# A decoder block in fp32 on one core: the gate of the last 512 output columns moves from the sum into the weights

## The chip, the cores and the metric

The kernel runs on one core of a Trainium2 chip. The metric is the device time of one execution in microseconds (us). The engines that matter here are TensorE (PE), VectorE (DVE), ScalarE (ACT), GpSimd (POOL) and the queue that issues most transfers, SyncE (SP).

## The reference, cut to what matters

One decoder layer with a convolution mixer and an MLP, all in float32, for 256 tokens of width 2048. The change touches only the last line of the MLP:

```python
h = _rms_norm(x, norm2_g[i]) * (1.0 + sc2[:, None, :]) + sh2[:, None, :]
u = jnp.square(jax.nn.relu(h @ mlp_w1[i]))        # 256 x 8192
x = x + (1.0 + g2[:, None, :]) * (u @ mlp_w2[i])  # gate row (1 + g2) per output column
```

The gate `1 + g2` is one row of 2048 numbers, the same for every token, so it may multiply the product `u @ w2` column by column, or the columns of `w2` ahead of the product.

## The kernel before, in words

**Precision.** Each weight tile arrives in SBUF as float32 in a buffer called `raw` (128 x 2048, 1 MB, seven buffers). `split_w` (L225) cuts a tile into two halves of 128 x 1024. For each half ScalarE writes a rounded copy `hi` (L236), and VectorE writes the rest, `lo = raw - hi` (L240). There are six buffers of each, so ScalarE can start a half only when TensorE has done with the one six earlier. TensorE multiplies three times for one product: activations' high part by `hi`, the same by `lo`, activations' low part by `hi` (L310 to L312, and L376 to L378 in `mm_eight`).

**Quarters.** The 8192 hidden columns are worked in four quarters: an "up" stage (`w1`) and a "down" stage (`w2`) each. A quarter's down product has four blocks of 512 output columns (n = 0 to 3). In the last quarter blocks 0 and 1 are put together from seven products of half size (called `eight` jobs, m = 1 to 7) and jobs `down 1` and `down 3`. Blocks 2 and 3 are plain: jobs `down 4` and `down 5` make block 2, `down 6` and `down 7` make block 3, each job one half of the sum over hidden columns. A `down` job has two weight tiles (c = 0, 1), so four halves; an `eight` job has one tile, so two halves. The written order of jobs is `LAST_JOBS`: down 4, eight 1, down 6, eight 5, eight 7, eight 3, down 5, eight 6, eight 2, down 1, eight 4, down 3, down 7. Below they are d4, e1, d6, e5, e7, e3, d5, e6, e2, d1, e4, d3, d7.

**Order of the work.** The program is emitted job by job; the splits of a job are emitted one job ahead of its matmuls, as urgent work. A planner then orders the instructions of each engine by priority and by its own estimate of when each is ready; the hardware runs each engine's list in that order. Some orders are written out by `tc.issue_after`: the tasks of a job (`run_tasks`, L314: finishing sums, squaring the hidden values, half sums) go behind the last `lo` and `hi` emitted, and the adds of the `eight` jobs on whole raw tiles (L356) go behind the last `lo` before them.

**Hidden values.** The squared hidden values `u` of a quarter are split in the same way: ScalarE writes the high part (L251), VectorE the low part (L254). d5 needs the last of them.

**The gate.** The gate row lies in `cb` (the tile `cond`), spread over all partitions, from a transfer that is issued at 890.1 us. For blocks 0 to 2 `finish` (L446) adds the sum in PSUM to `y` (what earlier quarters gave), multiplies by the gate row (L458) and lets a GpSimd-issued DMA add it to the output (L460). Block 3 is the one with `n == ADDED`. Its `y` is multiplied by the gate and joined with the residual ahead of time (`scale_y`, L1166 and L1167); `finish` then multiplies the PSUM sum by the gate (L458), adds it to `y` (L462) and stores `y` through SP (L463). It runs once for each half of the tokens, t = 0 and t = 1. The last job d7 finishes t = 0 before it begins t = 1.

Of the kernel before, what the change touches and what calls it, by code (L numbers as in the profile page):

```python
# [12 lines left out]
ALU = mybir.AluOpType  # L13
PSUM = bass.MemoryType.PSUM

P = 128
# [4 lines left out]
QUARTERS = FF // D  # L21
# [60 lines left out]
ADDED = 3  # L82
# [5 lines left out]
def conv_block(ctx: ExitStack, tc: tile.TileContext, x, vec, dwq, c_row, mod_r, mod_t, mod_c, w_first, w_in, w_out, w1, w2, out):  # L88
    nc = tc.nc
# [41 lines left out]
    for i in range(2):  # L131
        p = ps.tile([P, 2, 2 * T], F32, name="mm", bufs=2)
        for n in range(2):
            at = 8 * i + 4 * n
            nc.tensor.matmul(p[:, n, :], ones[0:1, :], cond[0:1, at : at + 4, :], start=True, stop=True)
        nc.scalar.activation(cond[:, 8 * i : 8 * i + 8, :].rearrange("p k n -> p (k n)"), p.rearrange("p a b -> p (a b)"), AF.Silu)
    cb = cond.rearrange("p k n -> p (k n)")
    nc.scalar.activation(cz[:, :, 3], col("c", 0, KT), AF.Silu)
    state = {"used": 0}
# [74 lines left out]
    def take(key, hold=False):  # L214
        assert order[state["used"]] == key, (order[state["used"]], key)
        state["used"] += 1
        if not hold:
            release(home(key))
        return raw.pop(key)
# [5 lines left out]
    def split_w(key, engine, w=None):  # L225
        w = take(key) if w is None else w
        if key[:2] == ("up", 0) and key[2] < UNSCALED:
            shown[key] = w
        halves = []
        for h in range(2):  # L230
            ks = slice(h * HALF, (h + 1) * HALF)
            hi = wts.tile([P, HALF, P], F32R, name="hi", bufs=6)
            lo = wts.tile([P, HALF, P], F32R, name="lo", bufs=6)
            with tc.issue_after(state["silu"]) if key == ("out", 1, 1) else ExitStack():
                with tc.issue_after(state["part"]) if key[0] == "in" and "part" in state else ExitStack():
                    state["w_hi"] = nc.scalar.activation(hi, w[:, ks, :], AF.Copy).ins  # L236
            by = nc.vector if key == ("in", HELD, 0) and h == 0 else engine
            with tc.issue_after(state["e_end"]) if key[0] == "out" and engine is nc.vector else ExitStack():
                with tc.issue_after(state["part_sum"]) if key[0] == "in" and "part_sum" in state else ExitStack():
                    end = by.tensor_tensor(lo, w[:, ks, :], hi.bitcast(F32), op=ALU.subtract)  # L240
            if by is nc.gpsimd:
                state["pool"] = end.ins
            else:
                state["w_lo_of"] = state.get("w_lo_of", [end.ins])[-1:] + [end.ins]
                state["w_lo"] = end.ins
            halves.append((hi, lo))
        parts[key] = halves
# [75 lines left out]
    def split_seven(q, m):  # L323
        name = {1: "x", 5: "x", 6: "x", 4: "x", 7: "w", 3: "z", 2: "y"}[m]
        if m == 1:
            for n in "xw":
                for c in range(2):
                    chain[n, c] = take(("seven", q, n, c), True)
        if m in (7, 2):
            for c in range(2):  # L330
                n = "z" if m == 7 else "y"
                chain[n, c] = take(("seven", q, n, c), True)
        for c in range(2):
            if m in PLUS:
                with tc.issue_after(state["w_lo_of"][c]):
                    nc.vector.tensor_tensor(chain[name, c], chain[name, c], chain[PLUS[m], c], op=ALU.add)
            if m in (6, 4):
                release()
        for c in range(2):
            with behind(c):  # L340
                split_w(("seven", q, m, c), nc.vector, chain[name, c])
            if m in (7, 4):
                release()
            if c == 0:
                run_tasks()
# [4 lines left out]
    def split_eight(q, m):  # L350
        name = OPERAND[m]
        for n in {1: "xw", 7: "z", 2: "y"}.get(m, ""):
            chain[n] = take(half_tile(q, n), True)
        if m in PLUS:
            with tc.issue_after(state["w_lo"]):
                nc.vector.tensor_tensor(chain[name], chain[name], chain[PLUS[m]], op=ALU.add)  # L356
        if m in (6, 4):
            release()
        if m == 1:
            run_tasks()  # L360
        split_w(("eight", q, m), nc.vector, chain[name])
        if m in (7, 4):
            release()
        if m != 1:
            run_tasks()
# [80 lines left out]
    def finish(n, t, cs, p):  # L446
        at = slice(512 * n + cs.start, 512 * n + cs.stop)
        s = y[:, t, at]
        g = two().rearrange("p a t -> p (a t)")[:, cs]
        with tc.issue_after(state["y_end"].ins) if "y_end" in state else ExitStack():  # L450
            if (n, t) in MORE:
                m, op = MORE[n, t]
                nc.vector.tensor_tensor(g, p, kept_of[m], op=op)
                p = g
            if n < ADDED:
                nc.vector.tensor_tensor(g, p, s, op=ALU.add)
                p = g
            state["y_end"] = nc.vector.tensor_tensor(g, p, cb[:, at], op=ALU.mult)  # L458
        if n < ADDED:
            nc.gpsimd.dma_start(rows_out[:, t, at], g, accum_op=ALU.add)  # L460
            return
        state["y_end"] = nc.vector.tensor_tensor(s, s, g, op=ALU.add)  # L462
        nc.sync.dma_start(rows_out[:, t, at], s)  # L463

    def residual_out(n, b):
        with tc.issue_after(state["load"].ins):
# [246 lines left out]
    def ps_two():  # L713
        return ps.tile([P, 2, T], F32, name="acc", bufs=2)

    def two():
        return tmp.tile([P, 2, T], F32, name="two", bufs=6)
# [53 lines left out]
    for job in jobs:  # L771
        n = quota.get(job, 0)
# [5 lines left out]
        if job[:2] in LATE_GATE:  # L778
            n = LATE_GATE[job[:2]][job[2]]
# [25 lines left out]
    def splits(job):  # L805
        if job[0] == "eight":
            with urgent():
                split_eight(*job[1:])
            return
        if job[0] == "seven":  # L810
            with urgent():
                split_seven(*job[1:])
            return
        for c in range(2):
            if job + (c,) in parts_early:
                continue
            on_pool = job[0] == "in" or job in POOLED
            with urgent(), behind(c):
                split_w(job + (c,), nc.gpsimd if on_pool else nc.vector)
            if c == 0:  # L820
                state["next_hi"] = state["w_hi"]
                if job[0] in ("up", "down"):
                    with urgent():
                        run_tasks()
# [10 lines left out]
    p = ps.tile([P, 512], F32, name="small", bufs=1)  # L835
    for k2 in range(HALF):
        s = two()
# [4 lines left out]
        for j in range(2):  # L842
            g = (2 * k2 + j) % 4
            nc.tensor.matmul(p[32 * g : 32 * g + 32, 0:T], ones[:, 0:32], s[:, j, :], start=k2 < 2, stop=k2 >= HALF - 2)
    mods(by_col(0))
    with urgent():
        part = two()[:, 0, :]
        nc.scalar.activation(part, p[:, 0:T], AF.Copy)
        p = ps.tile([P, 512], F32, name="row", bufs=1)
# [8 lines left out]
    for _ in range(2):  # L858
        p = ps.tile([P, 2, 2 * T], F32, name="mm", bufs=2)
# [52 lines left out]
    for k in range(KT):  # L912
# [4 lines left out]
        if c == 0:  # L917
            n = two()
# [7 lines left out]
        if last:  # L926
            w = take(("first", k))
# [241 lines left out]
    rows_out = out.rearrange("(t p) d -> p t d", t=2)  # L1169
# [5 lines left out]
    for n, job in enumerate(jobs):  # L1175
# [51 lines left out]
        if kind == "out" and i > 0:  # L1227
            p = ps_two()
        elif not by_tokens(job):
            p = ps.tile([P, 2, 2 * T], F32, name="mm", bufs=2)  # L1230
# [38 lines left out]
        if n == KT - 3:  # L1269
            for key in cols_in:  # L1270
                w = take(key)
# [7 lines left out]
        if kind == "in":  # L1279
# [86 lines left out]
            for k2 in range(HALF):  # L1366
# [17 lines left out]
                with urgent():  # L1384
                    nc.gpsimd.tensor_tensor(e, pair_of(cvs, k2), spread(mu), op=ALU.subtract)
                    state["e_end"] = nc.vector.tensor_tensor(e, e, spread(r), op=ALU.mult).ins
                    for c in range(2):
                        k = 2 * k2 + c
# [17 lines left out]
        if kind == "out":  # L1406
# [4 lines left out]
            with urgent():  # L1411
                for c in range(2):
                    k = 2 * i + c
# [10 lines left out]
            a = two()  # L1424
            for c in range(2):
                k = 2 * i + c
# [27 lines left out]
        elif kind == "up":  # L1454
# [5 lines left out]
            if plain:  # L1460
                with urgent():
                    t2 = evac(p)
                    a = two()
                    nc.vector.tensor_tensor(t2, t2, spread(r2), op=ALU.mult)
                    for c in range(2):
                        at = 2 * i + c
# [19 lines left out]
        else:  # L1486
# [16 lines left out]
            if job == ("down", QUARTERS - 1, 3):  # L1503
                with tc.issue_after(state["w_lo"]):
                    for t in range(2):
                        at = slice(1536, 2048)
# [3 lines left out]
            for t, cs, p in sums.pop((kind, i // 2)):  # L1510
                at = slice(512 * (i // 2) + cs.start, 512 * (i // 2) + cs.stop)
                s = y[:, t, at]
# [69 lines left out]
```

## Time and profile before

| | us |
|---|---|
| median of 3 runs (lowest, highest) | 1067.75 (1067.61, 1067.9) |
| span of the profiled execution, first to last instruction | 1065.8 |
| TensorE busy in the span | 1048.6 (98%) |
| VectorE busy | 911.9 (86%) |
| ScalarE busy | 609.0 (57%) |
| GpSimd busy | 220.2 (21%) |

Of the profiled execution the span is the time that is known; the median of the runs is 1.95 us above it. A span counts from the first to the last instruction that the profiler records. Times in timelines are from the start of the span. Instructions of one engine that follow each other without a pause may be drawn together (x4).

### The profile page before, as it was taken

The page shows a single profiled execution, that of the slowest core. Times are in us where ns is not written, and L with a number is a line of the kernel's source. Part 1 is how long each engine was busy: PE and PEld are TensorE (multiplying, and loading weights), DVE is VectorE, ACT ScalarE, POOL GpSimd, SP SyncE. Part 2 cuts the span into 40 slices and gives each one's busy share as a digit, 9 for nine tenths or more (in the row PEclk, how much of TensorE's full clock was granted, in tenths as well). Part 3 has the DMA queues.
Part 4 walks back from the last instruction along what each step waited for, and adds up shares of the span by engine and source line. Part 5 has one row for each costly group of instructions (what it writes and reads, how often), then busy time and mean ns, then how long its engine had stood idle before and what let it go on. Part 6 is the DMA issues. An engine that isn't in the chain of part 4 may idle for free.

```text
span 1065.8 us, 15587 instructions
## 1 busy us (share of the span) xinstructions
PE 1048.6 (98%) x5844; PEld 867.4 (81%) x5844; DVE 911.9 (86%) x1176; ACT 609.0 (57%) x841; POOL 220.2 (21%) x153
## 2 busy tenths in 40 slices
PE   6999999999999999999999999999999999999998
PEld 3888886678699998888888888888888888888886
DVE  5767789998766889878879899899999899899896
ACT  4111298866775587444546575745566744657751
POOL 0000078989689262000000000000000000000001
PEclk8999999999999999999999999999999999999999
DMA  9999997997999977999994998693989795899753
GB/s 383 420 420 421 415 419 310 359 397 261 382 401 404 405 247 285 324 334 313 324 359 178 340 269 284 238 382 109 383 241 308 252 331 183 289 304 341 203 146 60
DMA packets 154334, 331.01 MB, mean 311 GB/s; under 512 B 88465, under 2 KB 114321, under 8 KB 119313
## 3 DMA queue, kind: packets, MB, share of 16 engines
q1 hardware_dynamic: 153248, 328.30, 84.8%
q0 software_dynamic: 864, 1.57, 1.1%
q8 instruction: 46, 0.75, 0.3%
q14 instruction: 30, 0.25, 0.1%
q10 hardware_dynamic: 146, 0.13, 0.0%
HBM read 313.71 MB, written 17.83 MB: 311 GB/s over the span
## 4 chain that ended last, share of the span: by engine, by line
PE 83%; DMA 10%; DVE 5%; ACT 1%; issue 1%; SPq 0%; DVEq 0%; ACTq 0%
PE mm L312 12%; PE mm L310 12%; PE mm L311 12%; DMA raw<-mod_c 9%; PE mm L268 6%; PE mm L269 3%; PE acc L265 3%; PE acc L264 3%; PE acc L266 3%; PE mm L1090 2%; PE row L576 2%; PE acc L485 2%; PE acc L486 2%; PE acc L484 1%; DVE raw L669 1%; DVE lo L240 1%
## 5 line engine op out<-in xcount | busy, mean ns | idle before, releaser
L236 ACT ACTIVATE hi<-raw 128x1024 fp32r<-128x1024 f32 x374 | 384.8, 1055 | 258.2 <-PE mm L312 127.6
L240 DVE TENSOR_TENSOR lo<-raw,hi 128x1024 fp32r<-128x1024 f32 x313 | 371.7, 1219 | 52.6 <-ACT hi L236 51.4
L240 POOL TENSOR_TENSOR lo<-raw,hi 128x1024 fp32r<-128x1024 f32 x61 | 153.6, 2549 | 31.1 <-ACT hi L236 31.1
L669 DVE SCALAR_TENSOR_TENSOR raw<-raw,cond 128x2048 f32<-128x2048 f32 x50 | 117.7, 2356 | 27.0 <-DMA raw<-mod_c 26.9
L460 POOL DMA_DIRECT2D out<-two x6 | 5.4, 902 | 641.6 <-DVE two L458 632.3
L311 PE MATMUL mm<-lo,u 128*128 128x512 f32 x320 | 124.5, 389 | 0.0
L312 PE MATMUL mm<-hi,u 128*128 128x512 f32 x320 | 124.0, 389 | 0.0
L310 PE MATMUL mm<-hi,u 128*128 128x512 f32 x320 | 123.8, 389 | 0.0
L312 PE MATMUL mm<-hi,hl 128*128 128x512 f32 x288 | 112.1, 389 | 0.0
L311 PE MATMUL mm<-lo,hl 128*128 128x512 f32 x288 | 112.0, 389 | 0.0
L310 PE MATMUL mm<-hi,hl 128*128 128x512 f32 x288 | 112.0, 389 | 0.0
L969 DVE SCALAR_TENSOR_TENSOR acc<-u,v,acc 128x256 f32<-128x256 f32 x230 | 91.5, 482 | 0.0
L268 PE MATMUL mm<-hl,hi 128*128 128x512 f32 x224 | 80.0, 401 | 0.0
L311 PEld LDWEIGHTS mm<-lo,u 128*128 128x128 f32 x320 | 60.1, 188 | 12.6
L312 PEld LDWEIGHTS mm<-hi,u 128*128 128x128 f32 x320 | 60.1, 188 | 12.5
L310 PEld LDWEIGHTS mm<-hi,u 128*128 128x128 f32 x320 | 60.1, 188 | 12.4
L873 PE MATMUL mm<-two,first 128*128 128x256 f32 x240 | 57.0, 392 | 8.5 <-ACT two L931 8.5
L264 PE MATMUL acc<-hl,hi 128*128 128x256 f32 x224 | 63.4, 283 | 0.0
L265 PE MATMUL acc<-hl,hi 128*128 128x256 f32 x224 | 63.4, 283 | 0.0
L266 PE MATMUL acc<-hl,lo 128*128 128x256 f32 x224 | 63.4, 283 | 0.0
L312 PEld LDWEIGHTS mm<-hi,hl 128*128 128x128 f32 x288 | 54.1, 188 | 11.3
L311 PEld LDWEIGHTS mm<-lo,hl 128*128 128x128 f32 x288 | 54.1, 188 | 11.2
(381 smaller groups left out, 2059.2 us busy)
## 6 DMA issues: line engine op xcount, KB each, us to landing
raw<-w SPq DMA_DIRECT2D x128, 1024.0 KB, 7.3
raw<-mod_c SPq DMA_DIRECT2D x64, 1024.0 KB, 9.7
raw<-mod_r SPq DMA_DIRECT2D x28, 1024.0 KB, 8.8
raw<-w_in SPq DMA_DIRECT2D x16, 1024.0 KB, 10.5
raw<-w_out SPq DMA_DIRECT2D x16, 1024.0 KB, 8.0
first<-w_first SPq DMA_DIRECT2D x15, 1024.0 KB, 19.8
u<-kept SPq DMA_DIRECT2D x24, 512.0 KB, 7.6
flat<-two SPq DMA_DIRECT2D x30, 256.0 KB, 6.9
```

The lines of the kernel that those rows point to most:

```text
L236: state["w_hi"] = nc.scalar.activation(hi, w[:, ks, :], AF.Copy).ins
L240: end = by.tensor_tensor(lo, w[:, ks, :], hi.bitcast(F32), op=ALU.subtract)
L264: nc.tensor.matmul(out_p, w, m[:, 0:T], start=begin, stop=False)
L265: nc.tensor.matmul(out_p, w, m[:, T : 2 * T], start=False, stop=False)
L266: state["mm_end"] = nc.tensor.matmul(out_p, lo[:, k % HALF, :], m[:, 0:T], start=False, stop=end)
L268: nc.tensor.matmul(p[:, c, :], hi[:, k % HALF, :], m, start=(k == 0), stop=(k == KT - 1))
L310: nc.tensor.matmul(p, p_hi, hi, start=begin, stop=False, skip_group_check=shared)
L311: nc.tensor.matmul(p, p_hi, lo, start=False, stop=False, skip_group_check=shared)
L312: nc.tensor.matmul(p, p_lo, hi, start=False, stop=end, skip_group_check=shared)
L669: end = nc.vector.scalar_tensor_tensor(w, w, 1.0, cb, op0=ALU.mult, op1=ALU.mult, accum_out=acc)
L873: step = nc.tensor.matmul(held[n][:, c, :], w[:, 2 * n + c, :], h, start=k == 0 and c == 0, stop=k == KT - 1, skip_group_check=True)
L969: end = nc.vector.scalar_tensor_tensor(out, s, w, acc, op0=ALU.mult, op1=ALU.add)
```

## The change

In `split_w` the four tiles of d6 and d7 in the last quarter (`key[2] // 2 == ADDED`) get one more VectorE instruction for each half: the half of the raw tile is multiplied, in place, by the gate row of block 3 (two stretches of 512 columns in a half of 1024), ahead of `hi` and `lo`. That makes eight new instructions of 128 x 1024. In `finish`, block 3 loses the multiplication: it adds PSUM to `y` in one instruction and stores it. `scale_y` stays, and so do blocks 0 to 2.

```diff
         halves = []
+        gated = key[:2] == ("down", QUARTERS - 1) and key[2] // 2 == ADDED
         for h in range(2):
             ks = slice(h * HALF, (h + 1) * HALF)
+            if gated:
+                m = w[:, ks, :].rearrange("p (k a) n -> p k (a n)", a=4)
+                gate_row = cb[:, 512 * ADDED :][:, None, :].to_broadcast([P, 2, 512])
+                nc.vector.tensor_tensor(m, m, gate_row, op=ALU.mult)
             hi = wts.tile([P, HALF, P], F32R, name="hi", bufs=6)
             lo = wts.tile([P, HALF, P], F32R, name="lo", bufs=6)
...
         at = slice(512 * n + cs.start, 512 * n + cs.stop)
         s = y[:, t, at]
+        if n == ADDED:
+            with tc.issue_after(state["y_end"].ins):
+                state["y_end"] = nc.vector.tensor_tensor(s, p, s, op=ALU.add)
+            nc.sync.dma_start(rows_out[:, t, at], s)
+            return
         g = two().rearrange("p a t -> p (a t)")[:, cs]
         with tc.issue_after(state["y_end"].ins) if "y_end" in state else ExitStack():
             if (n, t) in MORE:
                 m, op = MORE[n, t]
                 nc.vector.tensor_tensor(g, p, kept_of[m], op=op)
                 p = g
-            if n < ADDED:
-                nc.vector.tensor_tensor(g, p, s, op=ALU.add)
-                p = g
-            state["y_end"] = nc.vector.tensor_tensor(g, p, cb[:, at], op=ALU.mult)
-        if n < ADDED:
-            nc.gpsimd.dma_start(rows_out[:, t, at], g, accum_op=ALU.add)
-            return
-        state["y_end"] = nc.vector.tensor_tensor(s, s, g, op=ALU.add)
-        nc.sync.dma_start(rows_out[:, t, at], s)
+            nc.vector.tensor_tensor(g, p, s, op=ALU.add)
+            state["y_end"] = nc.vector.tensor_tensor(g, g, cb[:, at], op=ALU.mult)
+        nc.gpsimd.dma_start(rows_out[:, t, at], g, accum_op=ALU.add)
```

## Rows read from the trace of the kernel before

**Rows 1.** The page, part 2: busy tenths in 40 slices of the span
```profile
PE   6999999999999999999999999999999999999998
DVE  5767789998766889878879899899999899899896
```

**Rows 2.** Stages: from:to, length, busy us (instructions) by engine, granted clock, DMA
```profile
975.00:990.00 15.00, 15.00 (x68) 12.39 (x67) 13.77 (x21) 7.67 (x10) 0.00 (x0) 1.00 0.92 289
1000.00:1010.00 10.00, 10.00 (x46) 8.29 (x45) 8.61 (x8) 9.65 (x14) 0.00 (x0) 1.00 0.51 160
1040.00:1050.00 10.00, 10.00 (x46) 8.29 (x45) 9.50 (x13) 2.79 (x3) 1.75 (x2) 1.00 0.42 52
1050.00:1061.00 11.00, 11.00 (x49) 8.85 (x48) 4.33 (x7) 0.00 (x0) 1.75 (x2) 1.00 0.45 73
```

**Rows 3.** The chain that ended last, its end: start us, us, what
```profile
1060.88 0.24 PE mm L312
...
1061.14 0.70 DVE two L458
...
1061.87 0.69 DVE x L462
```

**Rows 4.** SP's timeline at the end, and the landing of that transfer
```profile
1062.59 0.36 SPq L463 DMA_DIRECT2D out<-x  x1
out<-x SPq DMA_DIRECT2D x1, 256.0 KB, 2.1
```

**Rows 5.** DVE groups by shape, 960 to 1067: count, busy us, mean ns, idle before
```profile
L240 DVE TENSOR_TENSOR lo<-raw,hi 128x1024 fp32r<-128x1024 f32 x44 | 52.3, 1218 | 6.0 <-ACT hi L236 5.7
L458 DVE TENSOR_TENSOR two<-mm,cond 128x512 f32<-128x512 f32 x2 | 1.4, 692 | 6.7 <-PE mm L312 6.7
```

**Rows 6.** DVE's timeline, 981 to 1014: start us, us, what [idle before, releaser]
```profile
981.98 0.69 DVE L428 TENSOR_TENSOR hl<-v,hl 128x512 fp32r<-128x512 f32 x1 [0.36 <-ACT hl L427]
...
984.77 1.23 DVE L240 TENSOR_TENSOR lo<-raw,hi 128x1024 fp32r<-128x1024 f32 x1 [0.29 <-ACT hi L236]
986.30 3.94 DVE L240 TENSOR_TENSOR lo<-raw,hi 128x1024 fp32r<-128x1024 f32 x3 [0.31 <-ACT hi L236]
990.16 2.28 DVE L356 TENSOR_TENSOR raw<-raw 128x2048 f32<-128x2048 f32 x1
...
999.33 4.63 DVE L240 TENSOR_TENSOR lo<-raw,hi 128x1024 fp32r<-128x1024 f32 x4
...
1012.28 1.28 DVE L254 TENSOR_TENSOR u<-two,u 128x512 fp32r<-128x512 f32 x2
```

**Rows 7.** ACT's timeline: a `hi` of d6, and two of d5
```profile
985.21 1.06 ACT L236 ACTIVATE hi<-raw 128x1024 fp32r<-128x1024 f32 x1 [0.47 <-PE mm L312]
...
1006.73 1.99 ACT L236 ACTIVATE hi<-raw 128x1024 fp32r<-128x1024 f32 x2
```

**Rows 8.** PE's timeline: first `lo` of d6, of e7; u's low part in d5
```profile
990.67 0.39 PE L311 MATMUL mm<-lo,u 128*128 128x512 f32 x1
...
1004.05 0.39 PE L377 MATMUL acc<-lo,hl 128*128 128x512 f32 x1
...
1015.61 0.62 PE L312 MATMUL mm<-hi,u 128*128 128x512 f32 x2
```

**Rows 9.** SP's timeline and landing time: the load of d6's second tile
```profile
965.41 0.33 SPq L212 DMA_DIRECT2D raw<-w  x1
raw<-w SPq DMA_DIRECT2D x1, 1024.0 KB, 10.3
```

**Rows 10.** DVE's and PE's timelines: the last `lo` of d7, and its use
```profile
1045.91 1.23 DVE L240 TENSOR_TENSOR lo<-raw,hi 128x1024 fp32r<-128x1024 f32 x1 [0.47 <-ACT hi L236]
...
1054.37 0.39 PE L311 MATMUL mm<-lo,u 128*128 128x512 f32 x1
```

**Rows 11.** POOL's timeline: the last adding transfer, and its landing
```profile
1055.87 0.88 POOL L460 DMA_DIRECT2D out<-two  x1 [3.59 <-issue]
out<-two POOLq DMA_DIRECT2D x1, 256.0 KB, 4.1
```

## The prediction

> **What bounds the kernel now.** I read the page's slices first: TensorE is at 9 tenths in every slice but the first and the last, and VectorE runs at 8 and 9 tenths near the end [rows 1]. Then the stages. From 975 to 1061 us TensorE is busy for the whole length of each one, at its upper clock level (granted clock 1.00), so no microsecond is lost there to a wait, and only something that makes TensorE wait can add time [rows 2]. VectorE has little room: 13.8 of 15 us, 8.6 of 10, 9.5 of 10, and it gets room only after 1050 (4.3 of 11) [rows 2]. Third, the end of the chain of waits: TensorE's last matmul ends at 1061.12; VectorE then multiplies PSUM by the gate row from 1061.14 and adds into `y` from 1061.87 [rows 3]; the store is issued at 1062.59 and lands 2.1 us later [rows 4]. So the time is TensorE's work to 1061.12 and a tail of two VectorE instructions and a transfer.
>
> **The change part by part.**
>
> *The tail loses one instruction.* Between the starts of the multiply and the add lie 1061.87 - 1061.14 = 0.73 us [rows 3]. In the new kernel the add reads PSUM and `y` and can start at 1061.14 itself. An instruction of that shape with an operand in PSUM takes 692 ns [rows 5], the add from SBUF 0.69 [rows 3], so the add gets no longer. The store and its landing move forward by the same amount. The term is -0.73 us. The same happens to t = 0, five microseconds earlier, off the path. What is late next is the last adding transfer of block 1, issued at 1055.87 and landed 4.1 us later, at about 1060 [rows 11]; the store's landing moves from 1064.7 to 1064.0, so some 4 us remain between them.
>
> *Eight multiplies are added to VectorE.* No row has this instruction, a multiply in place with a row read twice. The nearest is the `lo` subtraction: the same engine, 128 x 1024, two float32 operands from SBUF, 1218 ns [rows 5]. In a row of four, three starts take 4.63 - 1.23 = 3.40 us, so one instruction more costs 1.14 [rows 6]. The far bounds are nothing for all eight, if they fall into idle time, and 8 x 1.23 = 9.8 us, if each lay on the path. I take 1.14 each: 4.56 us for d6 and 4.56 for d7. None of it is on the path unless a `lo`, a `hi` or a low part of `u` reaches TensorE late. So I follow the lag.
>
> *d6.* Before, VectorE did d6's four `lo` from 984.77, and the next add (e5's) began at 990.16 [rows 6]: 5.39 us for 4 x 1.14 = 4.56, so 0.83 idle, with 0.29 in front of it. ScalarE's `hi` waited for TensorE's buffers [rows 7], so these gaps can be filled by multiplies. The gap of 0.36 at 981.98 [rows 6] can take the first multiply as well, because the load is there: issued at 965.41 for the second tile, landed 10.3 us later, at 975.7 [rows 9]. What is left is a lag of 4.56 - 0.83 - 0.29 - 0.36 = 3.1 us, or 3.4 if the first multiply does not use that gap. Behind the last `lo` of d6 stand e5's add, e5's `lo`, e7's add and so on, an order written into the code, and all move by this lag. Now the slack. d6's first `lo` ended at 986.0 and was wanted at 990.67 [rows 6, 8]: one multiply and one round trip ahead of it, 2.3 us, does not reach 4.7. e7's first `lo` ended at 999.33 + 1.23 = 1000.56 and was wanted at 1004.05 [rows 6, 8]: slack 3.49, just above the lag. The low part of `u` in d5 ended at about 1012.28 + 0.68 = 1012.96 and was wanted at 1015.61 [rows 6, 8]: slack 2.65. Part of the lag should be gone by then, but little, because ScalarE is busy 9.65 of 10 us from 1000 to 1010 [rows 2] and d5's `hi` [rows 7] come late with it. With 2.7 to 3.1 us of lag left, TensorE would wait 0.05 to 0.45 us. Against that, the planner sees the later `u` and has matmuls of d5 that need only `hi`, `lo` and the high part of `u`; I count 0.1 us. The ends are 0 and, with nothing absorbed, the second rival's price.
>
> The Trainium skill, in VectorE: DVE Perf Modes, section "The DRAIN you can't avoid", says that the next VectorE instruction doesn't start until the pipe of the one in front is empty. By that eight instructions would cost 1.23 each instead of 1.14, 0.7 us more for d6's stretch, a lag of 3.8 and a wait of some 1.15 us at `u`: 1067.75 - 0.73 + 1.15 = 1068.2, slower than before. The four `lo` that follow each other in 4.63 us disagree with it [rows 6]; I leave it as a part of the second rival, one chance in twenty.
>
> *d7.* Its four multiplies come after d5's stretch, when the lag has had ScalarE's idle time to shrink (2.8 of 10 us busy from 1040 on) [rows 2]. The last `lo` of d7 ended at 1045.91 + 1.23 = 1047.14 and is wanted at 1054.37 [rows 10]: slack 7.2, above all four multiplies (4.56) and what may remain of d6's. The sums of blocks 0 and 1 that stand between them get later by up to 4.6 us; VectorE is idle for 6.7 us after 1050, between the two last waits for TensorE [rows 5], and takes them there. Cost 0; without that cover the last adding transfer would land at 1060 + 4.6 = 1064.6, beside the end of the store.
>
> *Moved transfers.* The raw buffers of d6 come free 3 us later, so SP's next loads of weights go out later by up to that. These are for d1 and later jobs. The add and the store of the last block stay on the same engines, and the fewer `two` buffers only make room.
>
> *Sum*: the span 1065.8 - 0.73 + 0.1 = 1065.2. The runs lie 1.95 above the span, so 1067.75 - 0.63 = 1067.1.
>
> **The rivals.**
>
> 1. *The forecast*: 1067.1, from 1066.8 (no wait; a store that lands 0.2 earlier) to 1067.6 (a wait of 0.5).
>
> 2. *VectorE's lag reaches TensorE at e7 and d5* (the other side). With no gap used, all 4.56 us of d6's multiplies arrive at e7: a wait of 4.56 - 3.49 = 1.07, and then 4.56 - 2.65 - 1.07 = 0.84 at d5's low part of `u`, together 1.9. That gives 1067.75 - 0.73 + 1.9 = 1068.9. It decides from a lag of 2.65 + 0.73 = 3.4 us at `u`: there the gain is gone. For it speaks VectorE's full stretch and ScalarE's in rows 2; against it the gaps beside d6's `lo` and the planner's freedom in the order of matmuls.
>
> 3. *A multiply at the head of VectorE's list waits for its load.* ScalarE's `hi` used to be the first to need a raw tile. If the planner believes that the load of 965.41 lands sooner than the 10.3 us it took [rows 9] and places the multiply there, VectorE stands for some microseconds with everything behind it, on top of the lag: 2 us more than in the second rival, 1068.9 + 2 = 1070.9. Against it: half sums and transposes emitted ahead fill VectorE until 981, past the landing.
>
> 4. *The tail gain is taken back by another end.* If the sums of blocks 0 and 1 slip by 4.6 us or more, the last adding transfer ends where the store ended: 1067.75, no change. The 4 us between the two landings and VectorE's idle time after 1050 speak against it. [...]
>
> **How the numbers follow.** Chances: forecast 0.60, second rival 0.24, third 0.06, fourth 0.10. The predicted time is the forecast's 1067.1. The range runs from 1066.6 (the forecast's low end with the spread of the runs, 0.15 to each side) to 1069.0, which takes in the fourth rival and the second at its full price; the third and the worst of the second are left out. A difference of 0.2% is 2.1 us, about what a measurement can tell from no change: faster means below 1065.6, slower above 1069.9. No case reaches the first: 0.02. The second comes from the third rival and waits above 2.9 us in the second: 0.07. Within: 0.91.
>
> **What the new profile would show.** The tail: one VectorE add with PSUM as operand right behind the last matmul and nothing between it and the store; if that is missing, the first term is wrong. Eight multiplies of about 1.2 us on `raw`, four before about 993 and four between 1019 and 1045. e5's add 3 us later than now against TensorE's place; TensorE without idle time from 975 to its last matmul, or with a wait for VectorE at e7's first `lo` or d5's low part of `u`: a total over 0.73 us there makes the second rival right. A VectorE wait on a transfer in front of a multiply shows the third. If TensorE's last matmul ends where it does now and the time still doesn't fall, it is the fourth. A matmul count or a pace other than today's would make the whole argument wrong.

## The result, and the profile after

The change made the kernel slower. Its median is 1074.53 us (1073.99 to 1075.92, 5 runs) against 1067.75 (1067.34 to 1067.9, 5 runs) in the same job: a ratio of 1.0065, 95% interval 1.0054 to 1.0076. The forecast was 1067.1 us, with a range up to 1069.0. The profiled execution has a span of 1072.2 us where the kernel before had 1065.8, so 6.4 us are to be found in the two traces.

The groups on VectorE, 960 to 1075 us (count, busy us, mean ns, idle before), correspond to [rows 5]:

```profile
L245 DVE TENSOR_TENSOR lo<-raw,hi 128x1024 fp32r<-128x1024 f32 x44 | 51.8, 1214 | 1.0 <-ACT hi L241 1.0
L236 DVE TENSOR_TENSOR raw<-raw,cond 128x1024 f32<-128x1024 f32 x8 | 9.4, 1211 | 3.4 <-DMA raw<-w 3.4
...
L456 DVE TENSOR_TENSOR x<-mm,x 128x512 f32<-128x512 f32 x2 | 1.4, 692 | 4.5 <-PE mm L317 4.5
```

The eight multiplies (L236) are there and as long as a `lo`. The last block has one instruction with PSUM as operand (L456), and nothing stands between it and the store. In the second row is something that the kernel before did not have: 3.4 us in which VectorE waited for the load of weights. The same stages as in [rows 2]:

```profile
975.00:990.00 15.00, 12.45 (x53) 9.62 (x53) 15.00 (x21) 3.59 (x5) 0.00 (x0) 1.00 0.99 318
1000.00:1010.00 10.00, 10.00 (x46) 8.28 (x45) 9.79 (x9) 8.19 (x12) 0.00 (x0) 1.00 0.55 177
1040.00:1050.00 10.00, 10.00 (x46) 8.29 (x45) 9.98 (x11) 5.25 (x5) 0.00 (x0) 1.00 0.21 26
1050.00:1061.00 11.00, 11.00 (x51) 9.09 (x50) 9.67 (x15) 0.00 (x0) 1.75 (x2) 1.00 0.35 44
```

TensorE lost time in one stage only, the first: 53 matmuls in place of 68 [rows 2]. Behind it TensorE is full again, and VectorE, which had 6.7 of 11 us free after 1050, has 1.3. Two places follow from these rows.

**TensorE in d4.** VectorE's timeline (start us, us, what, [idle before, releaser]), then TensorE's:

```profile
970.45 0.68 DVE L1166 TENSOR_TENSOR pad<-acc,pad 128x512 f32<-128x512 f32 x1
974.55 2.36 DVE L236 TENSOR_TENSOR raw<-raw,cond 128x1024 f32<-128x1024 f32 x2 [3.42 <-DMA raw<-w]
976.82 0.69 DVE L259 TENSOR_TENSOR u<-cz,u 128x512 fp32r<-128x512 f32 x1
...
980.96 0.68 DVE L259 TENSOR_TENSOR u<-shz,u 128x512 fp32r<-128x512 f32 x1
```
```profile
981.70 0.50 PE L317 MATMUL mm<-hi,u 128*128 128x512 f32 x1 [2.46 <-DVE u L259]
```

Up to 970.45 both executions agree to 0.01 us. Then the order in the instruction list decides: the first two multiplies of d6 stand ahead of the low parts of `u` that d4 needs, and their load hasn't landed. In the kernel before, these two low parts began at 971.32 and 975.46; now at 976.82 and 980.96, 5.5 us later: 3.42 of waiting and 2.27 for two multiplies, less the 0.20 that VectorE waited there before. The two in the kernel before:

```profile
971.32 0.69 DVE L254 TENSOR_TENSOR u<-cz,u 128x512 fp32r<-128x512 f32 x1 [0.20 <-ACT u L251]
...
975.46 0.68 DVE L254 TENSOR_TENSOR u<-shz,u 128x512 fp32r<-128x512 f32 x1
```

TensorE waits for the low part. The last block's add, which follows the last matmul at once, begins at 1064.35; VectorE's first instruction behind that matmul began at 1061.14 before [rows 3]. That is 3.2 us, and the fifteen missing matmuls at 0.23 each (3.4) agree as far as such counts can tell. The trace marks 2.46 of it as one wait, at the second low part; the rest is a short wait at the first and the starts behind both.

**Behind the last matmul.** The last adds of VectorE, and GpSimd's issues of the adding transfers:

```profile
1051.92 0.68 DVE L466 TENSOR_TENSOR two<-two,cond 128x512 f32<-128x512 f32 x1
...
1058.43 0.69 DVE L466 TENSOR_TENSOR two<-two,cond 128x512 f32<-128x512 f32 x1
...
1064.35 0.69 DVE L456 TENSOR_TENSOR x<-mm,x 128x512 f32<-128x512 f32 x1 [4.52 <-PE mm L317]
```
```profile
1052.97 0.87 POOL L467 DMA_DIRECT2D out<-two  x1 [13.04 <-DVE two L466]
1057.96 0.89 POOL L467 DMA_DIRECT2D out<-two  x1 [4.13 <-DVE two L463]
1062.25 0.87 POOL L467 DMA_DIRECT2D out<-two  x1 [3.40 <-issue]
1066.74 0.88 POOL L467 DMA_DIRECT2D out<-two  x1 [3.62 <-issue]
```

All four sums of blocks 0 and 1 are done by 1059.12, but their transfers leave one by one, 4.3 to 5.0 us apart, the last at 1066.74, after the store's add. From it to the end of the span are 5.46 us; before, the last one was issued at 1055.87 [rows 11] and the store ended the kernel. The span now ends 7.85 us after the start of the last block's add, before 4.66 after the start of its multiply: 3.2 us more, where the removed instruction should have made it 0.73 less. The chain of waits names it, towards its end:

```profile
1058.85 3.39 issue
...
1062.26 0.86 POOL out L467
1063.12 3.60 issue
```

So 6.4 = 3.2 (TensorE) + 3.2 (end), as the two traces are compared at the last add. On the path at the end is the chain of transfers alone, and the two parts are not independent: that chain starts with block 0's first sum, and VectorE's standstill in d4 makes that late as well. In the kernel before, that sum and the issue behind it were:

```profile
1040.69 0.68 DVE L458 TENSOR_TENSOR two<-two,cond 128x512 f32<-128x512 f32 x1
```
```profile
1041.73 0.87 POOL L460 DMA_DIRECT2D out<-two  x1 [10.23 <-DVE two L458]
```

The experiments test whether these are two causes, and what each is.

### The profile page after: what moved, and what is told of

The parts are those of the page before. It is cut to its first block, busy times and chain, and to the rows that moved or that the text cites. A ratio compares the mean times of both kernels' runs of the same rounds, so it can differ in the third digit from the quotient of the medians.

```text
span 1072.2 us, 15587 instructions
## 1 busy us (share of the span) xinstructions
PE 1049.4 (98%) x5844; PEld 867.4 (81%) x5844; DVE 918.7 (86%) x1182; ACT 607.8 (57%) x841; POOL 220.0 (21%) x153
## 4 chain that ended last, share of the span: by engine, by line
PE 73%; DVE 11%; DMA 9%; issue 3%; ACT 2%; SPq 0%; POOL 0%; POOLq 0%; DVEq 0%; ACTq 0%
PE mm L315 10%; PE mm L316 10%; PE mm L317 10%; DMA raw<-mod_c 7%; PE mm L273 6%; DVE lo L245 4%; PE mm L274 3%; PE acc L270 3%; PE acc L269 3%; PE acc L271 3%; PE mm L1094 2%; PE row L580 2%; DVE raw L673 1%; DVE raw L341 1%; PE acc L489 1%
## 5 line engine op out<-in xcount | busy, mean ns | idle before, releaser
L315 PEld LDWEIGHTS mm<-hi,hl 128*128 128x128 f32 x288 | 54.1, 188 | 11.3
L317 PEld LDWEIGHTS mm<-hi,hl 128*128 128x128 f32 x288 | 54.1, 188 | 11.3
```

Source lines behind the costliest of these rows:

```text
L315: nc.tensor.matmul(p, p_hi, hi, start=begin, stop=False, skip_group_check=shared)
L317: nc.tensor.matmul(p, p_lo, hi, start=False, stop=end, skip_group_check=shared)
```

## The experiments

All times are medians with lowest and highest, the ratio is to the kernel before in the same job (1067.65 to 1067.79 there). It rests on all runs and not on the two medians, so it can differ a little from theirs.

| run | what differs from the changed kernel | us | ratio, 95% |
|---|---|---|---|
| tail_only | no multiplies | 1066.91 (1066.65 to 1068.2) | 0.9994 (0.9985 to 1.0003) |
| only6 | multiplies on d6 alone | 1070.87 (1068.61 to 1071.97) | 1.0024 (1.0014 to 1.0033) |
| only7 | multiplies on d7 alone | 1070.59 (1069.64 to 1071.83) | 1.0026 (1.0016 to 1.0035) |
| hold6 | d6's each behind the newest `lo` | 1074.46 (1074.09 to 1075.12) | 1.0065 (1.0052 to 1.0077) |
| hold67 | as hold6; d7's behind block 0's sums | 1071.64 (1071.27 to 1074.95) | 1.0047 (1.0034 to 1.0061) |
| hold6u | d6's behind `u`'s low parts | 1073.23 (1069.99 to 1075.2) | 1.0046 (1.0033 to 1.006) |
| hold6u7 | as hold6u; d7's behind block 0's sums | 1067.71 (1067.29 to 1069.92) | 1.0001 (0.9992 to 1.001) |
| poolmul | multiplies on GpSimd | 1080.98 (1078.88 to 1081.66) | 1.0118 (1.0104 to 1.0131) |
| scratch | GpSimd's ring of transfers 1024 bytes, not 512 | 1075.67 (1074.32 to 1077.82) | 1.0077 (1.0064 to 1.0089) |
| before_shift | kernel before, ring and padding of scratch | 1073.2 (1073.11 to 1075.15) | 1.0057 (1.0043 to 1.007) |
| before_pad | kernel before, padding of scratch alone | 1072.97 (1072.73 to 1073.11) | 1.005 (1.0033 to 1.0067) |

**tail_only.**

```diff
-        gated = key[:2] == ("down", QUARTERS - 1) and key[2] // 2 == ADDED
+        gated = False
```

> The changed kernel without its eight multiplies (so block 3 of the last quarter gets no gate in this quarter's sum; that part is left out). VectorE's work ahead of the tail is then that of before. Theory and rival agree on the tail term: one VectorE instruction fewer behind the last matmul, 1067.75 - 0.73 = 1067.0 us, the last matmul ending at 1061.1 as before. If the gain is below 0.3 us, the store was not what ended the kernel before.

1066.91, that is 0.76 below the kernel before of its job (1067.67), though the interval of the ratio takes in 1. VectorE's timeline at the end shows the add alone behind the last matmul, and the span is 1065.2, so the store ends the kernel 3.9 us after the start of the add (4.66 after the start of the multiply before):

```profile
1061.32 0.69 DVE L456 TENSOR_TENSOR x<-mm,x 128x512 f32<-128x512 f32 x1 [4.75 <-PE mm L317]
```

The gain of the tail is there in the trace, and its 0.76 by the medians is near the 0.73 that was counted; the eight multiplies cost all the rest.

**only6 and only7.** The multiplies of one job are left out; only7 has `== 7` in this line.

```diff
-        gated = key[:2] == ("down", QUARTERS - 1) and key[2] // 2 == ADDED
+        gated = key[:2] == ("down", QUARTERS - 1) and key[2] == 6
```

> Only tile d6's weights are multiplied by the gate row; d7's are not, so half of the last block's product lacks the gate row: the output differs, the rest of the work is as after. Theory (two causes that add up: d6's first multiply waits 3.4 us for its load in front of u's low parts, +3.2 us for TensorE; d7's four multiplies push block 0's sums back and with them the chain of adding transfers, +3.9 us at the end less 0.7): the wait of 3.4 us and TensorE's 2.5 us in d4 are still there, the last matmul ends at 1064.3, the sums come some 4.6 us earlier than in after, and the store ends the kernel again: 1070.2 us. Rival (the sums are late because of the lag from d6, not of d7's multiplies): the adding transfers still end the kernel: 1072.5 us or more.

> Only tile d7's weights are multiplied by the gate row; d6's are not, so half of the last block's product lacks the gate row: the output differs, the rest is as after. Theory: nothing stands ahead of u's low parts in d4, TensorE ends at 1061.1 as before; block 0's first sum comes 4.6 us later than before, at 1045.3, and four adding transfers 4.4 us apart from there are issued by 1059.7 and end no later than the store: 1067.0 us (up to 1068). Rival (d7's four multiplies alone make the sums so late that the adding transfers end the kernel, as in after): 1070 us or more.

Each job's multiplies cost some 3 us by themselves: 3.1 for d6's and 2.8 for d7's over the 1067.79 of their job, each with the tail's gain of 0.76 already in it. Without it, 3.84 + 3.56 = 7.4, and the changed kernel has 6.78 + 0.76 = 7.54 (medians in all cases): two causes whose times add up. In only6 TensorE waits for `u`'s low part, and the last adding transfer is issued at 1057.90, early enough that the store ends the kernel; this was the theory. The wait differs between the two profiles with the landing of the load: VectorE waited 2.44 us here and 3.42 in the changed kernel. That may be why only6's runs spread over 3.4 us; this profile is of one of its shortest (1069.05). TensorE's waits in only6, in total, times, longest:

```profile
PE mm L317 <- DVE u L259: 1.9, 1, 1.9
```

For only7 the theory named the right mechanism and gave it the wrong size; the rival was right. TensorE waits for nothing from 960 on, and yet the kernel is 2.8 us slower. VectorE's first sum of block 0, then GpSimd's issues:

```profile
1049.00 0.68 DVE L466 TENSOR_TENSOR two<-two,cond 128x512 f32<-128x512 f32 x1
```
```profile
1050.04 0.87 POOL L467 DMA_DIRECT2D out<-two  x1 [13.46 <-DVE two L466]
1054.65 0.89 POOL L467 DMA_DIRECT2D out<-two  x1 [3.74 <-DVE two L466]
1058.90 0.87 POOL L467 DMA_DIRECT2D out<-two  x1 [3.37 <-issue]
1063.22 0.88 POOL L467 DMA_DIRECT2D out<-two  x1 [3.45 <-issue]
```

The sum that I expected at 1045.3, the old 1040.69 plus four multiplies, comes at 1049.00. The multiplies account for 4.6 of the 8.3 us. The rest is order: the planner now places the last three `lo` instructions (3.4 us) and `scale_y`'s first two instructions (L1170, at 1047.79, 1.2 us) ahead of that sum, where they stood behind it. That is 9.2 us of work in all, a part of which went into idle time. From the sum on, four transfers follow each other at the pace of GpSimd's queue.

**hold6 and hold67.** Two attempts to give the multiplies another place.

```diff
+                with tc.issue_after(state["w_lo"]) if key[2] == 2 * ADDED else ExitStack():
                     nc.vector.tensor_tensor(m, m, gate_row, op=ALU.mult)
```

In hold67 d6's are as here, and d7's are issued after `state["y_end"].ins`, which is the last of block 0's two sums at that point.

> The changed kernel with the four multiplies of d6 held behind e1's last lo on VectorE, so that none stands at the head of VectorE's list while its load is still under way. Theory (two causes: a multiply that waits 3.4 us for its load, and sums of blocks 0 and 1 so late that the adding transfers, one every 4.4 us, end the kernel): TensorE's wait at d4 goes (last matmul at 1061.1 to 1061.5 instead of 1064.3), but the sums stay late, so the end falls by about 3.4 us, not by 6.8: 1071 us, from 1070 to 1072. Rival (VectorE has no room for 9.1 us of new work, wherever it stands, and TensorE waits for the lag): TensorE still ends at 1063 or later, 1073 us or more.

> As hold6, and d7's four multiplies are held behind the sums of block 0 (behind the gate multiply of its second token half). Same instructions, same count. Theory: TensorE does not wait, block 0's sums are done by about 1046 us and the last adding transfer ends by about 1065, beside the store: 1067.0 to 1068.5 us. Rival (no room on VectorE): d7's lo then come too late for TensorE, which waits 3 us or more before its last job: 1071 us or more.

hold6 took the load wait away and won nothing: the theory's number fell. This order sets `lo` and multiply in turn, and each `lo` now waits for ScalarE's `hi`, which waits for the multiply in front of it. VectorE's timeline, then what TensorE waited for (lines are one higher in this kernel):

```profile
991.12 1.22 DVE L237 TENSOR_TENSOR raw<-raw,cond 128x1024 f32<-128x1024 f32 x1
993.47 1.23 DVE L246 TENSOR_TENSOR lo<-raw,hi 128x1024 fp32r<-128x1024 f32 x1 [1.12 <-ACT hi L242]
...
998.09 2.28 DVE L362 TENSOR_TENSOR raw<-raw 128x2048 f32<-128x2048 f32 x1
```
```profile
PE acc L382 <- ACT hi L242: 1.7, 1, 1.7
PE acc L383 <- DVE lo L246: 0.8, 1, 0.8
PE row L383 <- DVE lo L246: 0.7, 1, 0.7
```

e5's add comes at 998.09, 7.9 us later than before [rows 6], and TensorE loses 3.2 us between 1000 and 1010: the place of the prediction's second rival, at a higher price. hold67 keeps this loss (its three waits add up to 3.2 as well) and yet is 2.8 us faster than hold6. There the first sum of block 0 ends at 1044.86, and the last adding transfer is issued at 1063.29, not 1067.26. The end can therefore be mended apart from TensorE's loss.

**hold6u and hold6u7.** hold6u is the order that the prediction had in mind for d6.

```diff
+                with tc.issue_after(state["lo_end"]) if key[2] == 2 * ADDED else ExitStack():
                     nc.vector.tensor_tensor(m, m, gate_row, op=ALU.mult)
```

`lo_end` is the newest low part of an activation. hold6u7 has `state["y_end"].ins` for d7 in addition.

> d6's multiplies are issued behind u's low parts, when their load has landed; d7's are as in after. This is the order that the prediction had in mind for d6. Theory: the load wait of 3.4 us goes and with it TensorE's 2.5 us in d4; the last matmul ends at 1061.1 to 1061.6; block 0's first sum comes some 3.4 us earlier than in after, at 1048.5, the last adding transfer is issued at about 1062.7 and still ends the kernel: 1070 us (1069 to 1071.3). Rival (the lag of four multiplies reaches TensorE at e5 or e7 whatever stands behind them, the prediction's second way): TensorE waits there for lo by 1.7 us or more: 1072.5 us or more.

> d6's multiplies behind u's low parts (as in hold6u) and d7's four behind block 0's sums. Both waits that the runs so far point to are then gone: the load wait in front of u's low parts, and the late chain of adding transfers. Theory: TensorE keeps only the 1.2 us that hold6u showed between 1000 and 1010 (VectorE's lag of four multiplies at e5 and e7), block 0's sums come at 1041 to 1045, the store ends the kernel: 1067.0 + 1.2 to 2.0 = 1068.6 us (1068 to 1069.5). Rival (d7's multiplies, moved later, now hold up d7's own low parts): TensorE waits for lo in d7's job at 1043 to 1055 and the time is 1070.5 us or more.

In hold6u the load wait is gone and TensorE's wait at `u` shrinks to 0.2 us. But TensorE waits between 1000 and 1010, at a `lo` of e7 and a `hi` of d5:

```profile
1005.46 0.50 PE L382 MATMUL acc<-lo,hl 128*128 128x512 f32 x1 [0.38 <-DVE lo L245]
1009.03 0.73 PE L315 MATMUL mm<-hi,u 128*128 128x512 f32 x2 [0.78 <-ACT hi L241]
```

It has 38 matmuls there in place of 46, so 1.8 us are lost by the count and 1.2 by the waits. e7's add begins 3.7 us later than in only7, which has no multiplies in d6 (1000.71 against 996.37, less 0.66 by which this execution was late at 971 already). Not all of that need come from the multiplies. VectorE, then ScalarE, in front of `u`'s first low part, and the `lo` of e7:

```profile
974.51 0.69 DVE L259 TENSOR_TENSOR u<-cz,u 128x512 fp32r<-128x512 f32 x1 [2.44 <-ACT u L256]
...
1004.18 4.63 DVE L245 TENSOR_TENSOR lo<-raw,hi 128x1024 fp32r<-128x1024 f32 x4
```
```profile
971.33 0.63 ACT L545 ACTIVATE two<-two 128x512 f32<-128x512 f32 x1 [2.67 <-DMA two<-flat]
```

Here VectorE stands until 974.51, because ScalarE's `u` is late, behind a transfer that ScalarE waited for (`two<-flat`); in the changed kernel it stood until 974.55 for the load. That wait comes and goes between profiles: VectorE waited 0.20 us for this `u` in the kernel before and in hold6, 1.54 in only7, 2.09 in hold67 and 2.60 in hold6u7. So this profile, of one of hold6u's longer runs (1074.7), has another standstill where the load wait was, and up to 2.2 us of its lag behind the kernel before may be that one; no run separates the two.

The theory's early sum didn't come either: block 0's first is at 1052.03, where 1048.5 was expected and the changed kernel has 1051.92, and VectorE is busy for nearly all of the time from 975 on in both. Both theories for hold6u hold in part: TensorE's loss is smaller than in hold6, above the 0.5 that I allowed, and the last adding transfer, issued at 1067.40, still ends the kernel. With runs from 1070.0 to 1075.2 the median alone would not have told.

hold6u7 settles the end. With block 0's sums ahead of d7's multiplies, the time is that of the kernel before: 1067.71 against 1067.65. VectorE's and GpSimd's rows at the end of its profile:

```profile
1042.18 0.69 DVE L466 TENSOR_TENSOR two<-two,cond 128x512 f32<-128x512 f32 x1
...
1044.84 4.62 DVE L236 TENSOR_TENSOR raw<-raw,cond 128x1024 f32<-128x1024 f32 x4
```
```profile
1043.23 0.87 POOL L467 DMA_DIRECT2D out<-two  x1 [8.14 <-DVE two L466]
...
1061.31 0.88 POOL L467 DMA_DIRECT2D out<-two  x1 [3.62 <-issue]
```

All eight multiplies are in it, none before its load, and block 0's sums begin at 1042.18 and 1044.23, close to the 1040.69 and 1044.77 of the kernel before. TensorE doesn't wait in d7, so the rival fell. This profile is of the longest of its eleven runs (1069.92) and has the same two waits between 1000 and 1010 as hold6u, and the same late `u` ahead of them. The other ten lie between 1067.29 and 1067.93; how much of the waits they had isn't known, and the theory's 1068.6 was some 0.9 too high. One thing in this profile can explain a part of the 0.8 us that remain above tail_only: the add of t = 0 comes only 1.8 us before that of t = 1 (5.4 in tail_only), so the two stores go out close together, and the kernel ends 4.46 us after the start of the last add, not 3.88. That this costs the other runs as much isn't shown.

**poolmul.**

```diff
-                nc.vector.tensor_tensor(m, m, gate_row, op=ALU.mult)
+                nc.gpsimd.tensor_tensor(m, m, gate_row, op=ALU.mult)
```

> All eight multiplies on GpSimd, which has little to do in the last quarter, in place of VectorE. VectorE's list is then that of the version with the tail alone (1066.9). Theory (all of the loss came from what stood behind the multiplies on VectorE): 1066.9 us, no wait of VectorE or TensorE in d4, the sums of block 0 at 1040 to 1041. A GpSimd subtraction of this shape took 2.5 us, so the eight take some 20 us of an idle engine. Rival (GpSimd at work slows VectorE's subtractions beside it, or the adding transfers, which GpSimd issues, come late behind its multiplies): VectorE's low parts get longer than 1.14 us while GpSimd multiplies, TensorE waits for lo: 1068.5 us or more.

The slowest of all, 13.2 us above the kernel before. VectorE's instructions and their order are those of tail_only, but look at their lengths while GpSimd multiplies. GpSimd's row, then VectorE's:

```profile
975.89 11.03 POOL L236 TENSOR_TENSOR raw<-raw,cond 128x1024 f32<-128x1024 f32 x4 [566.01 <-DMA raw<-w]
```
```profile
975.23 4.54 DVE L245 TENSOR_TENSOR lo<-raw,hi 128x1024 fp32r<-128x1024 f32 x2
979.69 2.56 DVE L430 TENSOR_TENSOR v<-cz,v 128x256 f32<-128x256 f32 x1
...
984.65 2.82 DVE L259 TENSOR_TENSOR u<-shz,u 128x512 fp32r<-128x512 f32 x1
987.40 1.21 DVE L245 TENSOR_TENSOR lo<-raw,hi 128x1024 fp32r<-128x1024 f32 x1
```

An addition of 128 x 256 took 2.56 us here and 0.41 in the changed kernel, the low part of `u` 2.82 and 0.68: about one GpSimd multiply (11.03 / 4 = 2.76) each, as if the two engines took turns. From 987.40, with GpSimd done, the lengths are the usual ones. TensorE waited 8.6 us for `u`'s low part. The Trainium skill states in SBUF — State Buffer, section "Who interferes with whom", that a VectorE instruction with two inputs in SBUF and a GpSimd instruction that reads SBUF contend, and calls the ports that they share an exclusive lock. These rows agree with it.

Not all of the time is waiting: TensorE's waits add up to 10.2 us, and its last add comes 14.6 us later than in tail_only (1075.95 against 1061.32). Behind the long wait it ran at the lower of its two clock levels (1.2 GHz, granted 0.50), with matmuls 0.43 us apart and not 0.23:

```profile
985.00:990.00 5.00, 2.47 (x6) 0.50 0.04 18
```

The rival of this experiment had the mechanism; its "1068.5 us or more" lies far below what came.

**scratch, before_shift and before_pad.** If the adding transfers leave singly because their ring of descriptors is small, a larger one lets them go when their sums are there.

```diff
-PADDING = 560
+PADDING = 512
...
-    nc = bacc.Bacc("TRN2", target_bir_lowering=False, num_devices=1, dynamic_dma_scratch_size=512)
+    nc = bacc.Bacc("TRN2", target_bir_lowering=False, num_devices=1, dynamic_dma_scratch_size=1024)
```

The padding makes room for the ring. Each engine's list is that of the changed kernel.

> The changed kernel with a descriptor ring for GpSimd's transfers of 1024 instead of 512 bytes (and 192 bytes less of unused padding to make room); every engine's list of instructions is that of the changed kernel. Theory: the adding transfers no longer wait for one another (their starts now lie 4.3 to 4.5 us apart), the last one starts right behind the last sum at 1059.1 and lands by 1064, and the store ends the kernel: the end falls by 3.9 us to 1070.6 us, with TensorE's wait of 3.2 us still there. Rival (the transfers are slow for another reason, such as the adding itself, or the end is TensorE's wait alone): 1074 us, the starts still 4.4 us apart.

The transfers did as the theory says, each soon after its sum, as little as 1.3 us apart:

```profile
...
1061.54 0.89 POOL L467 DMA_DIRECT2D out<-two  x1 [2.33 <-DVE two L466]
1062.87 0.87 POOL L467 DMA_DIRECT2D out<-two  x1 [0.44 <-DVE two L466]
1064.93 0.86 POOL L467 DMA_DIRECT2D out<-two  x1 [1.19 <-DVE two L466]
```

The store ends the kernel again, 3.94 us after the start of its add (1069.96, span 1073.9): 3.9 less than in the changed kernel. But the total rose, because TensorE was slower over half of the kernel: 438 and 439 matmuls in 500 to 600 and 600 to 700 us, where the changed kernel has 441 and 442, and 436 from 800 to 900, where it has 442, all at the upper clock level (granted 1.00). Two controls without the change told why:

> The kernel before with the ring of GpSimd's transfers at 1024 bytes in place of 512 and the padding of the weight buffers at 512 in place of 560: the same instructions in the same order, other addresses. Theory (the slower pace of TensorE in scratch from 450 us on, 438 matmuls in 100 us in place of 442, comes from the addresses): the same pace here, and the last matmul some 5 us later: 1072.5 us (1071 to 1074). Rival (it has another cause in scratch): 442 matmuls per 100 us and 1067.7 us.

> The kernel before with only the padding ahead of the last pool of buffers at 512 columns in place of 560 (the ring as it was): the last pool, which holds the weights' and activations' halves of the last half of the kernel, lies 192 bytes further along in every partition. Theory (TensorE's pace hangs on where these buffers lie): 438 matmuls in 100 us from 450 us on, as in before_shift, and 1073 us. Rival (the larger ring slows it): 442 matmuls and 1067.7 us.

Both have the slower pace and the longer time; the padding is enough, and the ring has no part in it. TensorE in before_pad (442 and 443 matmuls in the kernel before):

```profile
500.00:600.00 100.00, 100.00 (x439) 1.00 0.83 290
...
800.00:900.00 100.00, 100.00 (x436) 1.00 0.82 274
```

The two also tell the ring from the padding at the end: the last two adding transfers are issued 4.46 us apart in before_pad, with the small ring (1056.46 and 1060.92), and 2.06 apart in before_shift, with the large one (1056.86 and 1058.92).

before_pad is 5.3 us slower than its kernel before. With that, scratch comes out: 1074.53 - 3.9 + 5.3 = 1075.9, measured 1075.67. The larger ring is worth what the theory said, and the addresses took more; this is a sum over runs, as none has the larger ring at the old addresses.

## Why the prediction was wrong

**The bound and the tail: right.** The time was TensorE's work and what follows it, and the tail lost its instruction for the 0.73 us that was counted: tail_only measured 0.76 by the medians, although the interval of the ratio includes 1.

**The price of a multiply: right.** 1.14 us each was taken; four in a row took 4.62 us, (4.62 - 1.21) / 3 = 1.14 from start to start. The rule that the prediction took from the Trainium skill, in VectorE: DVE Perf Modes, section "The DRAIN you can't avoid", that a VectorE instruction starts only when the pipe of the one before is empty, would have made it 1.21. The prediction left out that the same section lets a next instruction that is not held start earlier; the row, where the next starts 0.07 us before the end of the one in front, agrees with that exception.

**d6: wrong step.** "Half sums and transposes emitted ahead fill VectorE until 981, past the landing" was the ground on which the third rival got 0.06. It took the list of before as given and put the multiplies behind it. But the planner orders all of VectorE's work anew, and it put the first two at 971, ahead of `u`'s low parts, before the load had landed. The rival's mechanism came as described, and its price differed: TensorE lost 3.2 us at d4's low parts, and nothing at e7 and d5, where the rival had another 1.9; by then TensorE was late itself. In hold6u, without the load wait, TensorE lost 1.2 us by its waits (1.8 by the count) where the second rival had put 1.9, at e7 and d5; the forecast had 0.1. The slack of 3.49 at e7 was read rightly: in hold6u e7's first `lo` came 3.9 us later than before (1004.18 against 999.33, less 0.94 by which the execution was late at 971), and TensorE waited 0.38 for it. Whether the lag of 3.1 was too small for the multiplies stays open. The 3.9 hold VectorE's wait for a late `u`, up to 2.2 us more than before, a term that the prediction did not have.

**d7: wrong step.** "Some 4 us remain" and "cost 0". Two things failed. The sums of blocks 0 and 1 did not get later "by up to 4.6 us": block 0's first came 11.2 us later (1040.69 to 1051.92), and 8.3 with d7's multiplies alone, because other instructions were placed ahead of it. And VectorE's idle time after 1050 is a cover for the sums, not for what follows them. The four transfers form a chain of their own, 4.4 us from one to the next, and the chain starts with the first sum. Its sign stood in the prediction's own rows: the issue at 1055.87 had waited 3.59 us for "issue", not for VectorE [rows 11], while its sum, by the same trace, was done at 1053.05:

```profile
1052.36 0.69 DVE L458 TENSOR_TENSOR two<-two,cond 128x512 f32<-128x512 f32 x1
```

The right reckoning goes from the first sum: three steps of 4.4 us and 5.5 us from the last issue to the end. By that the old first issue at 1041.73 had, against the old end of the span, a slack of 1065.8 - 5.5 - 13.2 - 1041.73 = 5.4 us, so a first sum 8.3 us late moves the end by 2.9 and one 11.2 us late by 5.8; the spans of only7 (1068.8) and of the changed kernel (1072.2) moved by 3.0 and 6.4. The fourth rival had this place, and stopped at "no change"; its price is 2.8 us above the kernel before by itself (only7).

**The sum.** The forecast's 0.1 for d6 is 3.2, its 0 for d7 and the transfers 3.9, and -0.73 stands: 1067.75 + 3.2 + 3.9 - 0.7 = 1074.1, measured 1074.53. The third and fourth rivals came true at once, and the range of 1069.0 left that out. With the two orders mended, hold6u7 gave 1067.71, 0.6 above the forecast: its amount of work was about right, and its assumption on the order of that work was not. A version that beats both was not found. tail_only shows the most that such a change can bring here, 0.76 us or 0.07%, and none with all multiplies reached it.

## What to carry to other kernels

An instruction added to a full engine isn't only its length: find where in that engine's list the planner will put it, what stands behind it, and whether its own input can be late there; a load that only another engine waited for before becomes a wait of everything in that list. Where work slips, follow it to the transfers behind it, and look at how far apart one queue's issues stand and what they waited for: four transfers that go singly are a chain of their own, and slack is counted from its first link. Idle time of an engine near the end covers only what that engine itself does.

## What the runs showed of the hardware

GpSimd's adding transfers of 256 KB left 4.3 to 5.0 us apart in the changed kernel with a ring of 512 bytes, though their data lay ready, and 1.3 us apart at the least with 1024 (scratch). TensorE's pace hung on where buffers lie: with the padding ahead of the last pool smaller by 192 bytes in each partition, and nothing else changed, TensorE did 439 matmuls for 442 from 500 to 600 us and 436 for 443 from 800 to 900 at the same granted clock, and the kernel took 5.3 us longer (before_pad); by which mechanism is open. VectorE and GpSimd, each with two operands in SBUF, took turns for whole instructions, so that an instruction of 0.41 us became one of 2.56 (poolmul).
